# Hybrid attention block on one core: context exponentials of the global attention taken from PSUM under a running maximum, with query scaling, gate-weight rounding and context factors on POOL

## The chip, the core and the metric

The kernel runs on one core of a Trainium2 chip. The metric is the device time of one execution in microseconds, the median over several executions. A profiled execution gives a page and a trace; its span runs from the first to the last instruction.

## What is computed

The reference is one layer of a diffusion backbone with 1024 latent tokens, 256 context tokens and a model width of 1024. The latent tokens pass an input projection, three token mixers in parallel (windowed attention, branch 0; global attention, branch 1; a bidirectional recurrence, branch 2), a gated merge, an output projection and a feed-forward network. The change concerns the two attentions, most of all the global one. Each has 8 query heads in two groups of four that share a key and value head, a head width of 64, and 1280 keys for the global one: 256 of the context and then the 1024 latent ones.

```python
def dense_attn(q, k, v, sink=None):
    ...
    s = jnp.einsum('bqkgd,bjkd->bkgqj', q.reshape(B_, Lq, KV, G, hd), k).astype(jnp.float32) * hd ** -0.5
    ...
    p = jax.nn.softmax(s, axis=-1)[..., :k.shape[1]].astype(v.dtype)
    return jnp.einsum('bkgqj,bjkd->bqkgd', p, v).reshape(B_, Lq, HQ * hd)

def global_attn(q, k, v, ck, cv):
    ...
    k_all = jnp.concatenate([ck, k], axis=1)
    v_all = jnp.concatenate([cv, v], axis=1)
```

The gates of the merge are a plain projection of the normed tokens, 24 units of 128 output channels. The kernel computes them as filler work beside the other stages.

## The kernel before

All work is float32. A product of two float32 tensors is made from three matmuls: each operand is split into a rounded high part (`wh`, `hh`, `ph`, `KH`, written by a cast) and a low part, the difference (`wl`, `hl`, `pl`, `KL`, written by a subtraction on DVE).

The stages run one after another: modulation and norms, the recurrence (branch 2), the token-major projections, then the windowed attention, called stage A here (about 700 to 890 us of the span), the global attention, stage B (about 890 to 1210 us), then merge, output projection and feed-forward network. Stages A and B are one function, `attention`, called with `br` 0 and 1.

In each, a lead part loads keys and values (`prep`) and the first two queries (`qprep`). Then 16 iterations follow, one for each of 8 query tiles of 128 tokens and 2 head groups. In an iteration three generators are woven: `scores(it + 1)`, which makes the probabilities of the next iteration, `values(it)`, which multiplies the present ones with the values, and some steps of the gate units (`gz`, three matmuls a step). The names in the traces:

- `qf`, `qs`, `pq`, `QT`: a query tile as loaded, scaled and split, transposed in PSUM, and copied to SBUF.
- `sa` (stage A), `sbc` and `sbl` (stage B): scores in PSUM. In B, `sbc` holds the context scores of all four heads (128 x 1024) and `sbl` the latent scores of one head. Both take turns in the two buffers of one PSUM tag.
- `pw` in A, `pc` and `plat` in B: the exponentials. In A they are multiplied by the reciprocal sum on POOL (L1405). In B the reciprocal is broadcast to `yT_r` on POOL (L1446), turned by two matmuls into `pr`, copied to `ytmp_R` on ACT (L1316), and multiplied into the result `yT` (L1341).
- `pp`: four transposes of one key tile's probabilities into one PSUM bank. ACT casts it to `ph` (L1323), DVE subtracts to `pl` (L1324), and `po` accumulates values times `ph` and `pl` (L1305, L1306).
- `pq`, `pp` and `pr` take turns in the two banks of PSUM tag "a"; `po` and `gz` in those of tag "b".

In B, before the change, ACT copies the context scores from PSUM to `pc` as they are (L1424). When a head's latent maximum is known, DVE joins it with the context maximum (L1436), and ACT makes both exponentials under the common maximum (L1438 from PSUM, L1439 from `pc`). `values` goes through the two context tiles first and then through the eight latent ones.

A gate unit loads a weight (`wr`, 128 x 1024), ACT casts it to `wh` (L175), DVE subtracts to `wl` (L176). `wh` and `wl` have three buffers each.

The order on each engine is set when the program is built: a list scheduler takes priorities, buffers and its own costs, and so moves instructions of other engines too when one operation changes. At run time each engine goes through its list in order.

Of the kernel before, what the change touches and what calls it, by code (L numbers as in the profile page):

```python
# [12 lines left out]
AF = mybir.ActivationFunctionType  # L13
ALU = mybir.AluOpType
# [4 lines left out]
P = 128  # L19
# [72 lines left out]
def build(tc, ins, out, dbg=None):  # L92
    nc = tc.nc
    V, A, G, T, SP = nc.vector, nc.scalar, nc.gpsimd, nc.tensor, nc.sync
    with ExitStack() as top:
# [66 lines left out]
        cnt = [0]  # L162

        wprio = [0]

        def w_unit(src, nk, ncol, lo_eng=None):

            cnt[0] += 1
            n = nk * ncol
            with tc.high_priority(offset=wprio[0]):  # L170
                raw = wp.tile([P, 1024], F32, tag="wr", name=f"wr{cnt[0]}", bufs=WR)
                SP.dma_start(raw[:, :n] if len(src.shape) == 2 else raw[:, :n].rearrange("p (k n) -> p k n", k=nk), src)
                hi = wp.tile([P, 1024], F32R, tag="wh", name=f"wh{cnt[0]}", bufs=WH)
                lo = wp.tile([P, 1024], F32R, tag="wl", name=f"wl{cnt[0]}", bufs=WL)
                A.copy(hi[:, :n], raw[:, :n])  # L175
                (lo_eng or V).tensor_tensor(out=lo[:, :n], in0=raw[:, :n], in1=hi[:, :n].bitcast(F32),  # L176
                                            op=ALU.subtract)
            return (hi[:, :n].rearrange("p (k n) -> p k n", k=nk),
                    lo[:, :n].rearrange("p (k n) -> p k n", k=nk))
# [1046 lines left out]
def attention(tc, nc, ap_, br, ins, kv_d, q_d, y_d, mm2, bank, ident, identr, fill_gen, fill_steps):  # L1229
    V, A, G, T, SP = nc.vector, nc.scalar, nc.gpsimd, nc.tensor, nc.sync  # L1230

    def tl(shape, tag, nm, bufs=2, dt=F32):
        return ap_.tile(shape, dt, tag=tag, name=f"{tag}{br}_{nm}", bufs=bufs)
# [39 lines left out]
    def qprep(it):  # L1273

        tt, g = divmod(it, 2)
        qf = tl([P, 4, 64], "qf", f"q{it}")
        SP.dma_start(qf, q_d[tt][:, g * 256:(g + 1) * 256])
        qs = tl([P, 4, 2, 64], "qs", f"q{it}", dt=F32R)
        A.activation(qs[:, :, 0], qf, AF.Copy, scale=QSCALE)
        V.scalar_tensor_tensor(out=qs[:, :, 1], in0=qf, scalar=QSCALE, in1=qs[:, :, 0].bitcast(F32),  # L1280
                               op0=ALU.mult, op1=ALU.subtract)
        pq = bank("a", f"pq{br}{it}", (P, 4, P), F32R)
        for h in range(4):
            T.transpose(pq[:, h], qs[:, h].rearrange("p a b -> p (a b)"), identr)
        QT = tl([P, 4, P], "QT", it, 3, F32R)
        A.copy(QT, pq)
        QTs[it] = QT
# [8 lines left out]

    def values(it, PT, kts):
        tt, g = divmod(it, 2)
        Rs = None
        po = bank("b", f"po{br}{it}", (P, 4, P))  # L1300
        prev = []

# [3 lines left out]
            T.matmul(po, vv, pl, start=False, stop=n == len(kts) - 1)  # L1306

        for n, kt in enumerate(kts):
            if it in rs and n == 2:

                r = rs.pop(it)
                pr = bank("a", f"pr{br}{it}", (P, 2, P))
                for a in range(2):
                    T.matmul(pr[:, a], r[:, a * P:(a + 1) * P], ident, start=True, stop=True)
                Rs = tl([P, 2, P], "ytmp", f"R{it}")
                A.copy(Rs, pr)  # L1316
            pp = bank("a", f"pp{br}{it}{kt}")
            for h in range(4):
                T.transpose(pp[:, h], PT(h, n), ident)  # L1319
            ph = tl([P, 4, P], "ph", f"{it}{kt}", PV_BUF, F32R)  # L1320
            pl = tl([P, 4, P], "pl", f"{it}{kt}", PV_BUF, F32R)
            with tc.high_priority(offset=V_PRIO):
                A.copy(ph, pp)  # L1323
                V.tensor_tensor(out=pl, in0=pp, in1=ph.bitcast(F32), op=ALU.subtract)  # L1324
# [12 lines left out]
        for r in range(2):  # L1337
            sl = slice(r * 64, r * 64 + 64)
            V.tensor_tensor(out=yT[sl], in0=pv_[sl, :, r], in1=tmp[sl], op=ALU.add)
        if Rs is not None:  # L1340
            V.tensor_tensor(out=yT, in0=yT, in1=Rs, op=ALU.mult)  # L1341
# [69 lines left out]
def softmax_global(nc, tl, mm2, g, nm, QT, KH, KL, res, rs):  # L1411
# [1 line left out]
    V, A, G, T = nc.vector, nc.scalar, nc.gpsimd, nc.tensor  # L1413
    it = int(nm.split("_")[0])

    st = tl([P, 5, 4], "st", nm)
    nc_, ng, sm, r = st[:, 0], st[:, 1], st[:, 2:4], st[:, 4]
    pc = tl([P, 4, 256], "pc", nm)
    sc = mm2(f"sbc{nm}").rearrange("p a (b c) -> p (a b) c", b=2)
    for h in range(4):  # L1420
        T.matmul(sc[:, h], QT[:, h], KH[:, g, :256], start=True, stop=False)
        T.matmul(sc[:, h], QT[:, h], KL[:, g, :256], start=False, stop=True)
    V.tensor_reduce(out=nc_, in_=sc, axis=AX.X, op=ALU.max, negate=True)
    A.copy(pc, sc)  # L1424
    yield
    Pl = []
    for h in range(4):
# [11 lines left out]
        A.activation(pc[:, h], pc[:, h], AF.Exp, bias=n1, accum_out=sm[:, 0, h:h + 1])  # L1439
        Pl.append(pl)  # L1440
        if h < 3:
            yield
    V.tensor_tensor(out=r, in0=sm[:, 0], in1=sm[:, 1], op=ALU.add)
    V.reciprocal(r, r)
    rb = tl([P, 4, 64], "yT", f"r{nm}")
    G.tensor_copy(rb, r[:, :, None].to_broadcast([P, 4, 64]))  # L1446
# [127 lines left out]
```

## Time and profile before

| what | value |
| --- | --- |
| median of 3 runs | 2118.31 us (2118.1 to 2120.41) |
| the profiled execution's own time | 2119.41 us |
| its span | 2117.6 us |
| PE (matmuls) busy | 2078.3 us, 98% |
| DVE busy | 1379.4 us, 65% |
| ACT busy | 1003.0 us, 47% |
| POOL busy | 289.7 us, 14% |
| granted TensorE clock, mean | 0.996 |

A row of a group names line, engine, operation, output, inputs and shape, and then the durations. A row of a timeline has start, duration, engine, line and operation; in brackets stands how long the engine was idle before it and what released it. PE matmuls are pipelined: a 128x512 one reads 0.39 us in the rows, while the next starts about 0.23 us after it. So the starts, and not the durations, tell what PE needs.

### The profile page before, as it was taken

Reading aid. Unit: us, or ns where it says so; the run is one execution under the profiler, and the core shown is the slowest. Engines: PE = TensorE matmul, PEld = TensorE weight load, DVE = VectorE, ACT = ScalarE, POOL = GpSimd, SP = SyncE. Lnnn points to the kernel's source line nnn. Section 1 sums busy time; section 2 is a strip of 40 time slices with the busy share of each in tenths; the row PEclk is TensorE's granted clock in tenths of the full one; section 3 lists DMA queues with packets and bytes.
Section 4 is the critical chain, followed back from the end, with each engine's and each line's share of the span. In section 5 each row is a group of like instructions: output and inputs, shape, how many; then the busy total and the mean of one; then the engine's idle time right before and its main releaser. Section 6 shows DMA issues by size and latency. Waiting matters only on the chain.

```text
span 2117.6 us, 30402 instructions
## 1 busy us (share of the span) xinstructions
PE 2078.3 (98%) x11622; PEld 1735.2 (82%) x11622; DVE 1379.4 (65%) x2299; ACT 1003.0 (47%) x1760; POOL 289.7 (14%) x257
## 2 busy tenths in 40 slices
PE   7999999999999999999999999999999999999997
PEld 4888888888988788888888788888888888888887
DVE  4736756636565788677887747569777777664423
ACT  4333323311122877688888734346444444453322
POOL 0000000010022222100000000011333344100111
PEclk9999999999999999999999999999999999999999
DMA  9511111136644221211110454541322222295332
GB/s 364 205 44 36 46 50 32 50 113 201 195 139 134 85 60 53 81 45 33 36 33 28 133 188 147 192 151 49 100 86 84 90 71 89 80 304 192 108 124 85
DMA packets 95489, 229.66 MB, mean 108 GB/s; under 512 B 10736, under 2 KB 35696, under 8 KB 94320
## 3 DMA queue, kind: packets, MB, share of 16 engines
q1 hardware_dynamic: 95344, 227.72, 32.4%
q8 instruction: 91, 1.49, 0.3%
q14 instruction: 54, 0.44, 0.1%
HBM read 182.07 MB, written 45.61 MB: 108 GB/s over the span
## 4 chain that ended last, share of the span: by engine, by line
PE 69%; DVE 3%; ACT 2%; issue 1%; POOL 1%; DMA 1%; DVEq 0%; ACTq 0%; POOLq 0%; SPq 0%
PE pp L1319 5%; PE gz L199 3%; PE gz L200 3%; PE gz L201 3%; PE dn L929 3%; PE dn L930 3%; PE dn L928 3%; PE up L852 2%; PE up L853 2%; PE up L854 2%; PE po L1305 2%; PE po L1306 2%; PE br L200 2%; PE br L201 2%; PE br L199 2%; PE upc L854 2%
## 5 line engine op out<-in xcount | busy, mean ns | idle before, releaser
L175 ACT CAST wh<-wr 128x1024 fp32r<-128x1024 f32 (+1 forms) x139 | 145.1, 1045 | 397.7 <-PE dn L929 71.8
L176 DVE TENSOR_TENSOR wl<-wr,wh 128x1024 fp32r<-128x1024 f32 (+1 forms) x139 | 171.2, 1232 | 226.5 <-ACT wh L175 217.4
L1324 DVE TENSOR_TENSOR pl<-pp,ph 128x512 fp32r<-128x512 f32 x236 | 159.5, 688 | 30.4 <-ACT ph L1323 25.0
L199 PE MATMUL gz<-hh,wh 128*128 128x512 f32 x384 | 156.7, 409 | 2.8 <-ACT gs L523 2.8
L200 PE MATMUL gz<-hl,wh 128*128 128x512 f32 x384 | 152.8, 398 | 0.0
L201 PE MATMUL gz<-hh,wl 128*128 128x512 f32 x384 | 152.6, 398 | 0.0
L1323 ACT CAST ph<-pp 128x512 fp32r<-128x512 f32 x236 | 135.7, 585 | 33.6 <-PE pp L1319 31.1
L210 PE MATMUL tm<-wl,hh 128*128 128x256 f32 x384 | 109.0, 284 | 3.4 <-DVE wl L176 3.4
L211 PE MATMUL tm<-wh,hl 128*128 128x256 f32 x384 | 108.8, 283 | 0.0
L209 PE MATMUL tm<-wh,hh 128*128 128x256 f32 x384 | 108.8, 283 | 0.0
L1305 PE MATMUL po<-ph,VHL 128*128 128x512 f32 x236 | 106.4, 451 | 1.7 <-ACT ph L1323 1.1
L929 PE MATMUL dn<-ac,wh 128*128 128x512 f32 x256 | 99.7, 390 | 0.0
L930 PE MATMUL dn<-ac,wl 128*128 128x512 f32 x256 | 99.6, 389 | 0.0
L928 PE MATMUL dn<-ac,wh 128*128 128x512 f32 x256 | 99.6, 390 | 0.0
L1306 PE MATMUL po<-pl,VHL 128*128 128x512 f32 x236 | 98.0, 415 | 0.1
L199 PEld LDWEIGHTS gz<-hh,wh 128*128 128x128 f32 x384 | 73.0, 190 | 16.5 <-ACT gs L523 5.0
L201 PEld LDWEIGHTS gz<-hh,wl 128*128 128x128 f32 x384 | 72.9, 190 | 15.2
L200 PEld LDWEIGHTS gz<-hl,wh 128*128 128x128 f32 x384 | 73.2, 191 | 11.5
L210 PEld LDWEIGHTS tm<-wl,hh 128*128 128x128 f32 x384 | 73.7, 192 | 4.4 <-DVE wl L176 4.0
L1319 PE MATMUL pp<-ident,plat 128*128 128x128 f32 x512 | 77.1, 274 | 0.0
L1319 PEld LDWEIGHTS pp<-ident,plat 128*128 128x128 f32 x512 | 63.2, 141 | 17.0 <-DVE pl L1324 1.2
L733 ACT ACTIVATE u<-c,cw 128x1024 f32<-128x1024 f32 x38 | 47.3, 1246 | 61.9 <-DVE c L889 33.1
(1402 smaller groups left out, 5899.8 us busy)
## 6 DMA issues: line engine op xcount, KB each, us to landing
wr<-in_w_cm SPq DMA_DIRECT2D x48, 512.0 KB, 3.7
wr<-in_w_up SPq DMA_DIRECT2D x44, 512.0 KB, 3.6
wr<-in_w_down SPq DMA_DIRECT2D x33, 512.0 KB, 3.6
wmr<-in_w_mod SPq DMA_DIRECT2D x32, 512.0 KB, 4.6
gate_d<-gs SPq DMA_DIRECT2D x48, 256.0 KB, 2.0
sgt<-gate_d SPq DMA_DIRECT2D x24, 512.0 KB, 3.3
act_d<-u SPq DMA_DIRECT2D x22, 512.0 KB, 2.6
st<-act_d SPq DMA_DIRECT2D x44, 256.0 KB, 4.2
```

Of the source, the lines that this page charges most:

```text
L175: A.copy(hi[:, :n], raw[:, :n])
L176: (lo_eng or V).tensor_tensor(out=lo[:, :n], in0=raw[:, :n], in1=hi[:, :n].bitcast(F32), op=ALU.subtract)
L199: T.matmul(psl, wh[:, k, c], hh[:, k0 + k, cols], start=s, stop=False)
L200: T.matmul(psl, wh[:, k, c], hl[:, k0 + k, cols], start=False, stop=False)
L201: T.matmul(psl, wl[:, k, c], hh[:, k0 + k, cols], start=False, stop=e)
L210: T.matmul(psl, hh[:, k, toks], wl[:, k % 4, :], start=False, stop=False)
L928: T.matmul(z, w[0][:, c], h[0], start=s, stop=False)
L929: T.matmul(z, w[0][:, c], h[1], start=False, stop=False)
L930: T.matmul(z, w[1][:, c], h[0], start=False, stop=e)
L1305: T.matmul(po, vv, ph, start=n == 0, stop=False)
L1319: T.transpose(pp[:, h], PT(h, n), ident)
L1324: V.tensor_tensor(out=pl, in0=pp, in1=ph.bitcast(F32), op=ALU.subtract)
```

## The change

1. In stage B the context exponentials are made straight from the PSUM scores, under the context maximum alone (four instructions with their sums). The copy to `pc` and the later exponentials from `pc` are gone. When all four latent maxima are known, a factor `f`, the exponential of context maximum less common maximum, is made for four heads at once. POOL multiplies `pc` by it, DVE multiplies the context sums by it.
2. `values` in B goes through the eight latent tiles first and the two context tiles last.
3. In B, the broadcast reciprocal is turned at the end of `values`, and DVE multiplies `yT` with it from PSUM. The copy `ytmp_R` on ACT is gone.
4. In A and B, the scaled query is made on POOL instead of ACT.
5. For the 14 gate units that are the filler of stages A and B, the cast to `wh` runs on POOL instead of ACT. All other weights keep ACT.

```diff
@@ w_unit
-                A.copy(hi[:, :n], raw[:, :n])
+                if hi_on[0] is None:
+                    A.copy(hi[:, :n], raw[:, :n])
+                else:
+                    hi_on[0].tensor_copy(hi[:, :n], raw[:, :n])
@@ build, around the two calls of attention
+        hi_on[0] = G
         n0 = 10 + GATES_A
...
         hpool.close()
+        hi_on[0] = None
@@ qprep
-        A.activation(qs[:, :, 0], qf, AF.Copy, scale=QSCALE)
+        G.tensor_scalar(out=qs[:, :, 0], in0=qf, scalar1=QSCALE, scalar2=1.0, op0=ALU.mult, op1=ALU.mult)
@@ values
-            if it in rs and n == 2:
-
-                r = rs.pop(it)
-                pr = bank("a", f"pr{br}{it}", (P, 2, P))
-                for a in range(2):
-                    T.matmul(pr[:, a], r[:, a * P:(a + 1) * P], ident, start=True, stop=True)
-                Rs = tl([P, 2, P], "ytmp", f"R{it}")
-                A.copy(Rs, pr)
...
         for e in prev:
             pv(*e)
+        if it in rs:
+            r = rs.pop(it)
+            pr = bank("a", f"pr{br}{it}", (P, 2, P))
+            for a in range(2):
+                T.matmul(pr[:, a], r[:, a * P:(a + 1) * P], ident, start=True, stop=True)
+        else:
+            pr = None
...
-        if Rs is not None:
-            V.tensor_tensor(out=yT, in0=yT, in1=Rs, op=ALU.mult)
+        if pr is not None:
+            V.tensor_tensor(out=yT, in0=yT, in1=pr, op=ALU.mult)
@@ softmax_global
     V.tensor_reduce(out=nc_, in_=sc, axis=AX.X, op=ALU.max, negate=True)
-    A.copy(pc, sc)
+    for h in range(4):
+        A.activation(pc[:, h], sc[:, h], AF.Exp, bias=nc_[:, h:h + 1], accum_out=sm[:, 0, h:h + 1])
...
         A.activation(pl, sf, AF.Exp, bias=n1, accum_out=sm[:, 1, h:h + 1])
-        A.activation(pc[:, h], pc[:, h], AF.Exp, bias=n1, accum_out=sm[:, 0, h:h + 1])
...
-    V.tensor_tensor(out=r, in0=sm[:, 0], in1=sm[:, 1], op=ALU.add)
+    V.tensor_tensor(out=f, in0=ng, in1=nc_, op=ALU.subtract)
+    A.activation(f, f, AF.Exp)
+    for h in range(4):
+        G.tensor_scalar(out=pc[:, h], in0=pc[:, h], scalar1=f[:, h:h + 1], scalar2=1.0, op0=ALU.mult, op1=ALU.mult)
+    V.tensor_tensor(out=r, in0=sm[:, 0], in1=f, op=ALU.mult)
+    V.tensor_tensor(out=r, in0=r, in1=sm[:, 1], op=ALU.add)
     V.reciprocal(r, r)
...
-    res[it] = ((lambda h, n: pc[:, h, n * P:(n + 1) * P] if n < 2 else Pl[h][:, (n - 2) * P:(n - 1) * P]),
-               list(range(10)))
+    res[it] = ((lambda h, n: Pl[h][:, n * P:(n + 1) * P] if n < LT else pc[:, h, (n - LT) * P:(n - LT + 1) * P]),
+               [2 + n for n in range(LT)] + [0, 1])
```

How the instructions move, at three places. Lines of the changed kernel are some lines on: L1307 and L1308 are the two `po`, L1313 is `pp`, L1329 is `pr`, L1422 and L1423 are `sbc`, L1287 is `pq`, L203 is `gz`.

PE in stage B, at the end of an iteration, before (the last two latent tiles, `ph_78` and `ph_79`, of iteration 7, then the scores of iteration 9):

```order
L1305 MATMUL po_10369<-ph_78_10524,VHL_0_8531 128x512
L1421 MATMUL sbc__10570<-KH_0_8529,QT_9_10354 128x256
L1422 MATMUL sbc__10570<-KL_0_8530,QT_9_10354 128x256
...
L1306 MATMUL po_10369<-pl_78_10525,VHL_0_8531 128x512
L1305 MATMUL po_10369<-ph_79_10538,VHL_0_8531 128x512
L1284 MATMUL pq_10561<-identr,qs_q_10558 128x128 x2
L1306 MATMUL po_10369<-pl_79_10539,VHL_0_8531 128x512
L1284 MATMUL pq_10561<-identr,qs_q_10558 128x128 x2
L1421 MATMUL sbc__10570<-KH_0_8529,QT_9_10354 128x256
...
L1319 MATMUL pp_10582<-ident,pc_8__10357 128x128 x4
```

And with the change (iteration 6 ends with the context tiles `ph_60` and `ph_61`, then the scores of iteration 8):

```order
L1307 MATMUL po_10187<-ph_60_10343,VHL_0_8531 128x512
L1422 MATMUL sbc__10392<-KH_0_8529,QT_8_10169 128x256
L1423 MATMUL sbc__10392<-KL_0_8530,QT_8_10169 128x256
L1308 MATMUL po_10187<-pl_60_10344,VHL_0_8531 128x512
L1307 MATMUL po_10187<-ph_61_10357,VHL_0_8531 128x512
L1329 MATMUL pr_10367<-ident,yT_r__10100 128x128
L1308 MATMUL po_10187<-pl_61_10358,VHL_0_8531 128x512
L1329 MATMUL pr_10367<-ident,yT_r__10100 128x128
...
L1422 MATMUL sbc__10392<-KH_0_8529,QT_8_10169 128x256
L1423 MATMUL sbc__10392<-KL_0_8530,QT_8_10169 128x256
L1313 MATMUL pp_10407<-ident,plat_7_0_10223 128x128
```

Two of the eight `sbc` matmuls, where four were, now stand ahead of the last `po`; `pr` has come to this place; all four `pq` and six `sbc` stand between the last `po` and the first `pp` of the next iteration. In the odd iterations one more `sbc` and one `gz` stand there too.

ACT in stage B after that place, with the change (L1336 and L1337 copy `po`, L1289 is the copy `QT`, L1317 the cast `ph`, L1426 the new exponentials, L1440 a latent exponential):

```order
L1336 COPY ytmp_7_10587<-po_10406 64x256
L1337 COPY ytmp_7_10587<-po_10406 64x256
L1289 COPY QT_10_10604<-pq_10599 128x512
L1317 CAST ph_82_10628<-pp_10623 128x512
L1426 ACTIVATE pc_9__10607,st_9__10606<-sbc__10608,st_9__10606 128x256 x3
L1317 CAST ph_83_10640<-pp_10635 128x512
L1426 ACTIVATE pc_9__10607,st_9__10606<-sbc__10608,st_9__10606 128x256
L1317 CAST ph_84_10661<-pp_10656 128x512
L1440 ACTIVATE plat_9_0_10651,st_9__10606<-sbl_0_10644,st_9__10606 128x1024
```

Where one copy of the context scores stood, four exponentials now read them, and one `ph` stands between the third and the fourth.

POOL in stage A, iteration 3, with the change (L179 is the cast to `wh`, L1282 the scaled query, L1406 the product that makes `pw`):

```order
L1406 TENSOR_SCALAR pw_3_0_6581<-pw_3_0_6581,st_3__6575 128x640
L1406 TENSOR_SCALAR pw_3_1_6619<-pw_3_1_6619,st_3__6575 128x640
L179 CAST wh_7642<-wr_7640 128x1024
L1406 TENSOR_SCALAR pw_3_2_6646<-pw_3_2_6646,st_3__6575 128x640
L1282 TENSOR_SCALAR qs_q_7011<-qf_q_7009 128x4x64
L1406 TENSOR_SCALAR pw_3_3_6673<-pw_3_3_6673,st_3__6575 128x640
```

Before, the four L1405 stood there alone.

More of the change, by code (lines that the diff above doesn't have):

```diff
@@ L164, in build @@
         wprio = [0]
+        hi_on = [None]
         def w_unit(src, nk, ncol, lo_eng=None):
@@ L1298, in values @@
         tt, g = divmod(it, 2)
-        Rs = None
         po = bank("b", f"po{br}{it}", (P, 4, P))
@@ L1414, in softmax_global @@
     it = int(nm.split("_")[0])
-    st = tl([P, 5, 4], "st", nm)
-    nc_, ng, sm, r = st[:, 0], st[:, 1], st[:, 2:4], st[:, 4]
+    st = tl([P, 6, 4], "st", nm)
+    nc_, ng, sm, r, f = st[:, 0], st[:, 1], st[:, 2:4], st[:, 4], st[:, 5]
     pc = tl([P, 4, 256], "pc", nm)
```

## The prediction

> **What bounds the kernel now.** I read the page's busy line first, then busy time and PE's waits by stage, and then one period of stage B in order of time.
>
> ```profile
> PE 2078.3 (98%) x11622; PEld 1735.2 (82%) x11622; DVE 1379.4 (65%) x2299; ACT 1003.0 (47%) x1760; POOL 289.7 (14%) x257
> ...
> 700.00:890.00 190.00, 185.68 (x1090) 156.39 (x1090) 147.57 (x455) 144.54 (x361) 49.83 (x64) 1.00 0.20 60
> 890.00:1210.00 320.00, 316.95 (x1813) 259.07 (x1812) 252.91 (x420) 263.06 (x556) 6.44 (x16) 0.99 0.15 50
> ...
> PE pp L1319 <- POOL pw L1405: 1.5, 5, 0.6
> PE pq L1284 <- DVE qs_q L1280: 1.4, 1, 1.4
> PE po L1305 <- ACT ph L1323: 0.8, 1, 0.8
> PE gz L199 <- ACT gs L523: 0.5, 1, 0.5
> ...
> PE pr L1314 <- DVE pl L1324: 1.8, 4, 1.0
> ```
>
> The columns of a stretch are start and end, length, then the busy time of PE, PEld, DVE, ACT and POOL, the granted clock and DMA. PE is idle for 190 - 185.68 = 4.3 us of stage A and 320 - 316.95 = 3.05 us of B. In the lists of PE's waits (stage A above, B below) the named ones come to 4.2 us and about 2.5 us. ACT is busy 263 of 320 us in B and DVE 253: neither is full. So the 1.8 us or so that the change takes off ACT in a period of B is no gain by itself. Time comes only from PE's waits, from PE's own order, or it is lost to waits that the new order makes.
>
> ```profile
> 1002.65 0.29 PE L1284 MATMUL pq<-identr,qs_q 128*128 128x128 f32 x2
> 1002.78 0.47 PE L1306 MATMUL po<-pl,VHL 128*128 128x512 f32 x1
> 1003.08 0.29 PE L1284 MATMUL pq<-identr,qs_q 128*128 128x128 f32 x2
> 1003.21 0.35 PE L1421 MATMUL sbc__9929<-KH,QT 128*128 128x256 f32 x1
> 1003.40 0.27 PE L1422 MATMUL sbc__9929<-KL,QT 128*128 128x256 f32 x1
> 1003.51 0.28 PE L1421 MATMUL sbc__9929<-KH,QT 128*128 128x256 f32 x1
> ...
> 1003.75 0.60 PE L1319 MATMUL pp<-ident,pc__9716 128*128 128x128 f32 x4
> 1004.11 0.47 PE L199 MATMUL gz<-hh,wh 128*128 128x512 f32 x1
> 1004.42 0.39 PE L200 MATMUL gz<-hl,wh 128*128 128x512 f32 x1
> 1004.64 0.39 PE L201 MATMUL gz<-hh,wl 128*128 128x512 f32 x1
> ...
> 1007.38 0.68 PE L1314 MATMUL pr<-ident,yT_r__9861 128*128 128x128 f32 x4 [0.29 <-DVE pl L1324]
> 1007.82 0.48 PE L1305 MATMUL po<-ph,VHL 128*128 128x512 f32 x1
> ```
>
> Here I go by starts. A 128x512 matmul takes PE 0.22 to 0.23 us (1004.42 to 1004.64), four transposes 0.36 (1003.75 to 1004.11), a 128x256 one 0.11 to 0.12. The first 128x512 behind transposes takes 0.31 (1004.11 to 1004.42): a switch from transposes costs 0.31 - 0.22 = 0.09 us. The last row but one shows `pr` held by a bank that DVE had not yet left.
>
> ```profile
> 1003.28 0.37 ACT L1335 COPY ytmp<-po 64x256 f32<-64x256 f32 x1 [1.48 <-PE po L1306]
> 1004.06 0.59 ACT L1286 CAST QT<-pq 128x512 fp32r<-128x512 f32 x1
> 1006.21 1.01 ACT L1424 COPY pc__9928<-sbc__9929 128x1024 f32<-128x1024 f32 x1
> ...
> 1004.95 1.23 DVE L1423 TENSOR_REDUCE st__9927<-sbc__9929 128x4 f32<-128x1024 f32 x1
> 1006.21 0.42 DVE L1341 TENSOR_TENSOR yT<-yT,ytmp_R 128x256 f32<-128x256 f32 x1
> ...
> L1439 ACT ACTIVATE pc__8742<-pc__8742,st__8741 x4: 497/498/518, 906.0 to 912.7; 128x256 f32<-128x256 f32 x4
> L1316 ACT COPY ytmp_R<-pr x16: 370/373/378, 919.0 to 1195.2; 128x256 f32<-128x256 f32 x16
> L1279 ACT ACTIVATE qs_q<-qf_q x32: 410/421/463, 698.0 to 1116.7; 128x256 fp32r<-128x256 f32 x32
> L1446 POOL COPY yT_r__9009<-st__8859 x1: 403/403/403, 928.1 to 928.1; 128x256 f32<-128x256 f32 x1
> ...
> L1446 POOL COPY yT_r__11984<-st__11838 x1: 403/403/403, 1189.0 to 1189.0; 128x256 f32<-128x256 f32 x1
> ```
>
> This is ACT and then DVE in the same period. The broadcasts give the period: (1189.0 - 928.1) / 14 = 18.64 us.
>
> **The change part by part**, against the profiled execution of 2119.41 us.
>
> *ACT in B.* The copy (1.01), `ytmp_R` (0.37) and the query (0.42) go: 1.8 us a period. The four context exponentials stay, 0.50 each, with another source and place. The exponential of the factor is new, at most one of theirs. All of it lies beside PE and counts zero; were the cover gone, ACT's 263 us would have to reach 317.
>
> *Fewer switches.* The two orders have 119 and 199 switches from transposes to other matmuls in A and B before, 111 and 190 after. 17 fewer at 0.09: **-1.5 us**. Bounds 0 and -1.5.
>
> *`pr` at the end.* It no longer cuts in between the first tiles: the 1.8 us of its four waits go. One of these, 1.0, stands in the last iteration. **-1.8**, bounds -1.8 and 0.
>
> *Queries and `wh` on POOL, stage A.*
>
> ```profile
> L1405 POOL TENSOR_SCALAR pw<-pw,st__6724 128x640 f32<-128x640 f32 x4 | 3.2, 809 | 6.3 <-DVE st__6724 L1400 5.2 <-DVE st__6724 L1403 0.7 <-ACT ph L1323 0.4
> L1405 POOL TENSOR_SCALAR pw<-pw,st__8212 128x512 f32<-128x512 f32 x4 | 2.8, 700 | 7.3 <-PE sa L1389 4.1 <-DVE st__8212 L1403 3.3
> L581 POOL COPY tbA<-cs 128x512 f32<-128x512 f32 x2 | 1.2, 612 | 34.1 <-DMA cs<-in_rope 34.1
> L145 POOL CAST identr<-ident 128x128 fp32r<-128x128 f32 x1 | 0.3, 291 | 3.9 <-DMA ident<-in_ident 3.9
> L1137 POOL COPY S<-S x8: 614/1501/1512, 180.6 to 415.0; 64x512 f32<-64x512 f32 x8
> ```
>
> 809 less 700 ns for 128 more elements is 0.85 ns an element, so the scaled query of 256 is about 0.49 us. 612 less 291 for 384 elements is 0.84, so a `wh` cast of 1024 is about 1.04 us (estimates from these rows). Stage A gets 16 x 0.49 + 7 x 1.04 = 15 us on a POOL busy 49.8 of 190. Before the four products of an iteration POOL idles 6.3 us, 1.6 each, so one cast or query fits into each gap. `pp` waits for what is queued behind it, the third and fourth `pw`. If no gap were free, six casts in such places would cost up to 6 us; if ACT's relief brought `pw` earlier, the 1.5 us of waits would go. I take **-0.5**, near the second, since the gaps are longer than what is put into them.
>
> The wait of 1.4 us at the start of A is for the second query. Its load stands behind the key tiles, whose buffers ACT frees, and ACT loses the casts there. **-1.0**, bounds -1.4 and 0 (the transfer itself may set it).
>
> *The new order at the end of an iteration of B.* Call t0 the start of the last `po` (1002.78 above). The two `po` copies start 0.50 after it, `QT` starts at 1.28 and ends at 1.87. With the change PE needs behind t0: `po` 0.30, half of `pr` 0.22, four `pq` 0.26, six `sbc` 0.72; so it asks for the first `pp` at 1.5. The two "a" banks are then held by `pr`, until DVE's multiply at 1006.21 + 0.42, or t0 + 3.85, and by `pq`, until `QT`. So `pp` waits 1.87 - 1.5 = 0.37 us in even iterations, and about nothing in odd ones, where a `gz` and an `sbc` (0.35) come first. Ahead of t0, two `sbc` fewer (0.24) cover the last `pl`, which comes no earlier: on its way the factor and two small DVE operations take the place of one exponential. Against the waits before that is 0 to 0.6 us a period; I take 0.2, half of the one and a little of the other. 15 periods: **+3.0**, bounds 0 and +9.
>
> *The tail of B.* In the last iteration the scores have run out.
>
> ```profile
> 1190.00:1192.00 2.00, 1.09 (x6) 0.53 (x4) 1.66 (x2) 1.96 (x5) 0.00 (x0) 1.00 0.91 295
> 1192.00:1194.00 2.00, 1.68 (x7) 1.53 (x8) 1.96 (x5) 1.10 (x2) 0.00 (x0) 0.61 0.99 342
> 1194.00:1196.00 2.00, 2.00 (x8) 1.71 (x7) 1.79 (x3) 1.28 (x3) 0.00 (x0) 0.54 0.96 371
> ```
>
> PE was idle 0.91 us of two, then the granted clock was 0.61 and 0.54: 2 x 0.39 + 2 x 0.46 = 1.7 us lost. With the change ACT still casts a merge weight there while PE waits for `ph`, so I expect another idle gap and another dip. **-0.5**, bounds -1.7 (no dip) and +1.7 (twice as long).
>
> The Trainium skill, "TensorE: Matmul & The Clock Gate" (the HAM clock gate), says that the clock falls to half after an idle window of about 3.4 us. Here a gap far shorter went ahead of the fall, so the trace decides; by the rule alone the tail's clock would be an accident of the window, and this term zero.
>
> Sum: -1.5 - 1.8 - 0.5 - 1.0 + 3.0 - 0.5 = **-2.3 us**. The profiled execution lies 1.1 above the median of 2118.31, so on the median: 2116.0 us.
>
> **The rivals.**
>
> *The waits go and no new ones come.* PE's 7.3 us of idle time in A and B fall to some 3, `pw` and `QT` come early since ACT is freer, and the dip is gone: -4.3 - 1.5 - 1.7 = -7.5, about **2110.8**. For it: every named wait hangs on ACT or on what ACT delays. Against it: the new `pp` stands 0.37 us before its bank.
>
> *The context scores hold their bank too long: slower.* The second latent `sbl` needs the buffer that `sbc` leaves. Before, that was at 1006.21 + 1.01, t0 + 4.4. Now the reduction ends at t0 + 3.4 and three exponentials (1.5), a `ph` (0.59) and the fourth with its read-out (0.69) follow: t0 + 6.2. In even iterations PE asks for it after about 1.5 + 4.3 (two `pp` and a third 1.07, six `gz` 1.45, four `sbl` 0.92, switches and `po` 0.87) = t0 + 5.8. The wait at `pp` hides this 0.4; whatever else delays the reduction or ACT does not hide. At 0.7 us a period it costs 10.5: 2116.0 - 3.0 + 10.5 = **2123.5**. It turns the sign from about 0.35 us a period on (5.3 us of gains over 15). Against it: ACT has 1.8 us a period more room.
>
> *It changes nothing.* New and old waits balance: **2118.3**.
>
> *POOL and DVE get in each other's way.* L1137 has 64x512 copies of 1.50 us in the median beside one of 0.61: POOL was held 0.9 us. If the casts met that in stage A, `pw` would come 0.9 late in seven iterations, 6.3 us: **2122.3**. Against it: the L1405 rows of one shape stay within 809 and their like. The Trainium skill, "SBUF — State Buffer" (Who interferes with whom), has the rule: a DVE instruction with two SBUF inputs and a POOL instruction that reads SBUF block each other whole. That speaks against moving work to POOL beside `wl`; `pl`, with one input in PSUM, would be free.
>
> **How the numbers follow.** Forecast 0.46, with its own range 2113 to 2120; the first rival 0.26, the second 0.15, no change 0.09, the last 0.04. 0.2% is 4.2 us, about what a measurement tells from none: faster is below 2114.1, slower above 2122.5. A quarter of the forecast's chance lies below 2114.1: faster 0.26 + 0.11 = 0.37. Slower is the second rival and half of the last, 0.17; the rest, 0.46, is the same. The range, 2108 to 2124, leaves out the low end of the first rival and the high half of the second.
>
> **What would show it.** PE's waits in B no longer name `pr`; `pp` waits for `QT` in even iterations, `sbl` for L1426 at most 0.4 us. The period of B is 18.5 to 18.8 us. ACT's busy time in B falls by some 30 us and the span hardly moves. A `pw` that waits behind a cast, or PE waits in B above 6 us in sum, would make the prediction wrong upward; a clock of 1.00 at the end of B downward.

## The result and the profile after

The changed kernel takes 2123.86 us in the median of 9 runs (2121.4 to 2126.05), the kernel before 2119.12 (9 runs, 2117.51 to 2120.41). The ratio is 1.0026, with a 95% interval of 1.0017 to 1.0035: slower by about 5 us. I had forecast 2116.0, so the sign is wrong.

The profiled execution of the changed kernel took 2125.58 us, its span is 2123.8. First the busy line, then stages A and B with the columns of the prediction, then the longest named waits of PE in A (two rows) and in B (the rest).

```profile
PE 2077.6 (98%) x11622; PEld 1734.5 (82%) x11622; DVE 1392.6 (66%) x2331; ACT 961.5 (45%) x1698; POOL 348.7 (16%) x367
...
700.00:890.00 190.00, 184.44 (x1087) 157.09 (x1087) 153.91 (x455) 133.88 (x337) 65.48 (x85) 1.00 0.19 60
890.00:1210.00 320.00, 312.44 (x1791) 254.96 (x1790) 252.91 (x447) 231.43 (x517) 47.73 (x100) 1.00 0.15 47
...
PE pp L1313 <- POOL pw L1406: 4.9, 5, 1.0
PE po L1307 <- ACT ph L1317: 0.4, 1, 0.4
...
PE po L1307 <- ACT ph L1317: 1.8, 2, 1.0
PE pp L1313 <- DVE yT L1342: 1.5, 2, 1.2
PE pq L1287 <- DVE qs_q L1283: 0.8, 1, 0.8
PE pp L1313 <- ACT QT L1289: 0.8, 5, 0.2
PE pp L1313 <- DVE pl L1318: 0.7, 1, 0.7
PE sbl L1433 <- ACT plat L1440: 0.4, 1, 0.4
```

PE's work is the same (11622 instructions), its idle time is not: 5.6 us in A (4.3 before) and 7.6 us in B (3.05 before). ACT's busy time in B fell by 32 us, as expected, and bought nothing. In A the waits for `pw` went from 1.5 to 4.9 us. In B `pr` is gone from the list, and other names have come, five of them among the rows shown; with three smaller rows the list comes to 6.8 us, above the 6 that I had set as a sign against the forecast.

The first and the last context scores mark stage B for PE: the first two rows are the kernel before, the last two the changed one (of a tile's four matmuls, first and last start).

```profile
L1421 PE MATMUL sbc__8743<-KH,QT x4: 278/278/280, 900.4 to 901.6; 128*128 128x256 f32 x4
L1421 PE MATMUL sbc__11840<-KH,QT x4: 278/281/282, 1169.8 to 1171.2; 128*128 128x256 f32 x4
```

```profile
L1422 PE MATMUL sbc__8743<-KH,QT x4: 280/282/351, 902.4 to 903.4; 128*128 128x256 f32 x4
L1422 PE MATMUL sbc__11902<-KH,QT x4: 278/282/365, 1175.7 to 1177.7; 128*128 128x256 f32 x4
```

From 900.4 to 1171.2 are 270.8 us, from 902.4 to 1177.7 are 275.3: B is 4.5 us longer (4.6 to the very last matmul of the context scores). Its period, by the broadcasts on POOL, is (1196.4 - 932.1) / 14 = 18.88 us, 18.64 before. From the first transposed keys of A to B's first context scores it is 0.4 us more, behind B 0.3 less. The 1.8 us more before 40 us in this one profile are not the change's but a dip of the clock: from 15 to 20 us the granted clock is 0.66, and 1.00 in the kernel before. 2 of the 18 kernels below (x_qv, x_q13) show the same dip, 16 do not.

**How the table below is made.** For each matmul I took the time to the next start, less what its shape needs (128x512 0.227, 128x256 0.117, 128x128 0.108 us; the last of a group of transposes together with the one behind it; the transposes of `pq` need less than 0.108, so every kernel's sum is somewhat low). The sum between first and last context scores is PE's time beyond its work in B: 11.6 us before, 15.8 after. Pieces above 0.13 us I count as waits, what is left are small delays between matmuls of different kinds. The column "pw" is what the profile names as `pp` waiting for `pw` in A.

| kernel | what it has | ratio to before (95%) | pw, A | beyond work, B |
| --- | --- | --- | --- | --- |
| before | | 1 | 1.5 | 11.6 |
| changed | parts 1 to 5 | 1.0026 (1.0017 to 1.0035) | 4.9 | 15.8 |
| e1_ctx | 1, 2 | 1.0014 (1.0006 to 1.0023) | 1.5 | 14.8 |
| e2_pr | 3 | 1.0028 (1.0019 to 1.0036) | 1.5 | 17.0 |
| e3_pool | 4, 5 | 1.0018 (1.0010 to 1.0027) | 4.7 | 15.3 |
| e4_nopr | 1, 2, 4, 5 | 1.0054 (1.0042 to 1.0066) | 4.7 | 21.6 |
| e5_ctxpr | 1, 2, 3 | 1.0015 (1.0006 to 1.0024) | 1.5 | 15.8 |
| e6_q | 4 | 0.9995 (0.9984 to 1.0006) | 2.3 | 12.0 |
| e8_prb | all, `pr` in another bank | 1.0123 (1.0107 to 1.0138) | 4.7 | 35.0 |
| c1_slen | none, other order | 0.9995 (0.9986 to 1.0004) | 1.5 | 11.3 |
| x_nowh | 1 to 4 | 1.0003 (0.9994 to 1.0012) | 2.5 | 13.4 |
| x_qv | all, `QT` on DVE | 1.0018 (1.0009 to 1.0027) | 5.1 | 16.0 |
| x_q13 | 4, other order | 0.9996 (0.9987 to 1.0005) | 2.2 | 10.6 |
| x_a13 | all, other order | 1.0032 (1.0021 to 1.0044) | 4.7 | 17.6 |
| z_1in | all, sums with one tensor input | 1.0020 (1.0010 to 1.0029) | 3.4 | 15.7 |
| z_nowh_qv | 1 to 4, `QT` on DVE | 1.0000 (0.9991 to 1.0009) | 2.3 | 12.1 |
| z_nowh_qv_fold | the same, sink sum folded | 1.0009 (1.0000 to 1.0018) | 3.6 | 12.3 |
| z_q13_fold | 4, other order, fold | 0.9990 (0.9982 to 0.9999) | 3.7 | 11.2 |
| w_a | 1 to 4, and 5 for A | 1.0012 (1.0003 to 1.0021) | 3.6 | 14.6 |
| w_b | 1 to 4, and 5 for B | 1.0018 (1.0009 to 1.0027) | 4.3 | 15.8 |

Medians are of 4 to 12 runs each, beside 9 to 31 runs of the kernel before.

### The profile page after: what moved, and what is told of

Same layout as the page of the kernel before. It is cut to its first block, busy times and chain, and to the rows that moved or that the text cites. A ratio compares the mean times of both kernels' runs of the same rounds, so it can differ in the third digit from the quotient of the medians.

```text
span 2123.8 us, 30532 instructions
## 1 busy us (share of the span) xinstructions
PE 2077.6 (98%) x11622; PEld 1734.5 (82%) x11622; DVE 1392.6 (66%) x2331; ACT 961.5 (45%) x1698; POOL 348.7 (16%) x367
## 4 chain that ended last, share of the span: by engine, by line
PE 61%; DVE 2%; ACT 2%; issue 1%; DMA 1%; POOL 1%; DVEq 0%; SPq 0%; POOLq 0%; ACTq 0%
PE pp L1313 5%; PE dn L932 3%; PE dn L931 3%; PE dn L933 3%; PE up L855 2%; PE up L857 2%; PE up L856 2%; PE po L1308 2%; PE po L1307 2%; PE br L204 2%; PE br L205 2%; PE br L203 2%; PE gz L203 2%; PE gz L204 2%; PE gz L205 2%; PE upc L857 2%
## 5 line engine op out<-in xcount | busy, mean ns | idle before, releaser
L177 ACT CAST wh<-wr 128x1024 fp32r<-128x1024 f32 (+1 forms) x125 | 130.3, 1043 | 388.3 <-PE dn L932 70.4
L1317 ACT CAST ph<-pp 128x512 fp32r<-128x512 f32 x236 | 136.2, 586 | 59.8 <-PE pp L1313 58.6
L203 PE MATMUL gz<-hh,wh 128*128 128x512 f32 x384 | 156.2, 407 | 3.6 <-ACT gs L527 3.6
L1307 PE MATMUL po<-ph,VHL 128*128 128x512 f32 x236 | 105.4, 446 | 2.2 <-ACT ph L1317 2.2
L1308 PE MATMUL po<-pl,VHL 128*128 128x512 f32 x236 | 98.4, 417 | 0.4 <-DVE pl L1318 0.4
L203 PEld LDWEIGHTS gz<-hh,wh 128*128 128x128 f32 x384 | 72.8, 189 | 16.7 <-ACT gs L527 5.4
L204 PEld LDWEIGHTS gz<-hl,wh 128*128 128x128 f32 x384 | 72.7, 189 | 11.3
L1313 PE MATMUL pp<-ident,plat 128*128 128x128 f32 x512 | 78.1, 275 | 3.7 <-DVE yT L1342 1.5
L1313 PEld LDWEIGHTS pp<-ident,plat 128*128 128x128 f32 x512 | 61.4, 140 | 23.7 <-ACT QT L1289 4.8
L204 PE MATMUL br<-yl,wh 128*128 128x512 f32 x192 | 75.1, 391 | 0.3 <-DVE yl L1471 0.2
```

Source lines behind the costliest of these rows:

```text
L203: T.matmul(psl, wh[:, k, c], hh[:, k0 + k, cols], start=s, stop=False)
L204: T.matmul(psl, wh[:, k, c], hl[:, k0 + k, cols], start=False, stop=False)
L1307: T.matmul(po, vv, ph, start=n == 0, stop=False)
```

## The experiments

### Which part costs it

Parts 1 and 2, part 3, and parts 4 and 5, each put alone into the kernel before; and the changed kernel with part 3 undone. The edits are the hunks of the diff above, taken singly.

> Parts 1 and 2 alone (context exponentials from PSUM, factor, latents first); the reciprocal's turn stays early with its copy, queries and gate weights stay on ACT. In the changed kernel stage B lost 4.6 us from its first to its last context scores, stage A and its lead together about nothing. Theory 'turn at the end' (pr and pq hold both 'a' banks, pp waits for QT): this kernel has no turn there, so it should be at 2119 +- 1.5, ratio 1.000. Theory 'context part' (context tiles last, their bank held by four exponentials, the factor's small operations ahead of pl on DVE): the loss is here, 2122 to 2124, ratio 1.0015 to 1.0025. Theory 'POOL': 2119.

> Part 3 alone (turn of the reciprocal at the end of values, multiplied from PSUM). Theory 'turn at the end': a pp behind QT costs 0.3 us in each of 15 periods and takes the place of the old waits of pr, which were 1.8 us: 2121 to 2123, ratio 1.001 to 1.002. Theory 'context part': the four waits of pr go and nothing comes, 2117 to 2118.5, ratio 0.999. Theory 'POOL': the same 2117 to 2118.5.

> Parts 4 and 5 alone (scaled query and 14 gate weights on POOL). In the changed kernel pp waited 4.9 us for pw in stage A (1.5 before), the wait of 1.4 for the second query was gone, and the first query of stage B came 0.8 late. Theory 'turn at the end' and theory 'context part': these balance to +0 to +2, 2119 to 2121. Theory 'POOL': all of the loss, 2122.5 to 2124.5, with most of it in stage B, where queries on POOL come later.

> The changed kernel with part 3 undone: the turn is made early again, at the third key tile, and copied by ACT. Theory 'turn at the end': B's loss of 4.6 us goes, 2119 to 2120.5, ratio 1.000 to 1.0007. Theory 'context part': it stays, 2123 to 2125, ratio 1.002 to 1.003; the waits at the iteration's end change their names only. Theory 'POOL': it stays too.

No theory had this: each part alone is slower (1.0014, 1.0028, 1.0018), and their sum, 0.6%, is more than twice the whole, 0.26%. Undoing part 3 does not help, it doubles the loss (1.0054). With the context part and POOL's work in place (e4_nopr), `pr` at the early spot waits in 12 iterations, 7.3 us in sum, where the kernel before had 2.0. So part 3 is a loss alone and a gain beside the others; the parts can't be priced singly, and why part 3 alone costs so much was not followed up. Both theories that name one part for B fell.

### The POOL parts taken apart, and a control

```diff
 e6_q     (before, and only:)
-        A.activation(qs[:, :, 0], qf, AF.Copy, scale=QSCALE)
+        G.tensor_scalar(out=qs[:, :, 0], in0=qf, scalar1=QSCALE, scalar2=1.0, op0=ALU.mult, op1=ALU.mult)
 e5_ctxpr (changed, with the ACT query, and:)
-        hi_on[0] = G
+        hi_on[0] = None
 e8_prb   (changed, and:)
-            pr = bank("a", f"pr{br}{it}", (P, 2, P))
+            pr = bank("b", f"pr{br}{it}", (P, 2, P))
 c1_slen  (before, and:)
-S_LEN = 1.35
+S_LEN = 1.3
```

> Part 4 alone (scaled query on POOL). In the run with parts 4 and 5 alone DVE waited 11.1 us for POOL's scaled query in stage B (2.5 for ACT's before), with pl queued behind. Theory 'the query on POOL stalls DVE': this shows here again, some 10 us of DVE waits, B 3 to 5 us longer than before, 2120 to 2122. Rival 'the gate weights on POOL did it': B as before within 1 us, 2118 to 2119.

> Parts 1, 2 and 3 without the POOL parts 4 and 5; PE's list at the iterations' ends is that of the changed kernel. Theory 'the order at the end costs it': the pp waits of 0.2 to 0.3 us a period stay and B stays 3.5 to 5 us longer than before: 2121.5 to 2123.5. Rival 'the POOL parts cost it': B within 1.5 us of before, 2118 to 2120.

> The changed kernel with the turn of the reciprocal in a bank of the other tag, that of po and gz. In the changed kernel pp waited 0.23 to 0.32 us in 12 periods of stage B, 3.3 us in sum, while pr and pq held both 'a' banks. Theory 'a banks held': these waits go below 0.1 us each and the time falls by 3 us or so from the 2123.9 of the changed kernel, to 2120 to 2121.5 (ratio 1.0005 to 1.0013). Rival 'the bank only names the wait' (a wait for po or gz, which share their banks with pr then, takes its place): 2123 to 2126, ratio 1.002 to 1.0035.

> A control: the kernel before with one number of the weave altered (1.30 for 1.35, the share of steps that scores take), so the same instructions on the same engines in another order in stage B. Theory 'the old order is a narrow optimum' (any other order of B brings waits of 0.1 to 0.3 us a period): 2120 to 2123, ratio 1.001 to 1.002. Rival 'order does not matter at this size, the parts of the change do': 2118 to 2119, ratio 1.000.

The control is at 0.9995, and its PE list is another one in stage B: that the order differs is no loss by itself. The query on POOL is free, though DVE stands still for it as the theory said; this row is e6_q's, DVE's waits in B:

```profile
DVE qs_q L1283 <- POOL qs_q L1282: 13.9, 13, 3.3
```

13.9 us of waits of an engine with work behind them, and PE does not see them: the theory "the query on POOL stalls DVE" fell. e3_pool less e6_q leaves the gate weights: 0.23%. In e5_ctxpr the waits of `pp` at the iteration's end stay, and so does B's loss. e8_prb came out far worse than even its rival: `gz` and `po` now wait for DVE's `yT`, 3.5 and 2.4 us, and much else with them. The list of all engines is another, so it says nothing of the "a" banks.

### The gate weights off POOL; the wait for QT taken away

```diff
 x_nowh (changed, and:)
-        hi_on[0] = G
+        hi_on[0] = None
 x_qv   (changed, and:)
-        A.copy(QT, pq)
+        (A.copy if br == 0 else V.tensor_copy)(QT, pq)
 x_q13  (e6_q with S_LEN = 1.3)      x_a13  (changed, with S_LEN = 1.3)
```

> The changed kernel with part 5 undone: the 14 gate weights are cast on ACT again, the queries stay on POOL. Theory 'gate weights on POOL hold pw': pp's waits for pw in stage A fall from 4.9 us to between 1.5 and 2.5, A gets 2 to 3 us shorter, B stays some 4 us longer than before: 2121 to 2122, ratio 1.0010 to 1.0016. Rival 'the casts cost nothing': 2123 to 2124.5, ratio 1.002 to 1.003.

> The changed kernel with the copy QT of stage B on DVE instead of ACT, where it stands behind the two copies of po (0.37 each). Theory 'pp waits for a bank that QT leaves late': on DVE the copy (about 0.69, as pl of the same shape) can start as soon as the four pq are done, some 0.4 us earlier, and the 12 pp waits of 0.23 to 0.32 us shrink below 0.1: 2120.5 to 2122, ratio 1.0008 to 1.0016. Rival 'the pp wait only stands where other delays of the same place would be seen' (small pieces of pr, pq, sbc and po between one another, DVE's own queue): 2123 to 2126, ratio 1.002 to 1.0035.

> Part 4 alone (scaled query on POOL) together with the weave number 1.30 of the control: each of the two was at 0.9995 of before. If their gains are of separate places they add: 2116 to 2117.5, ratio 0.9985 to 0.9992. Rival 'one order's luck doesn't carry over to another': 2118 to 2120, ratio 0.9997 to 1.0006.

> The changed kernel with the weave number 1.30: the same instructions in another order in stage B; six or seven sbc still stand behind the last po in the even iterations, with four transposes of pq and one of pr. Theory 'the chain at the iteration's end (po, its copies, QT, pp) costs it whatever the weave': B stays 3.5 to 5.5 us longer than before, 2122.5 to 2125. Rival 'the loss is a bad draw of the scheduler': B within 2 us of before, 2119 to 2121.

x_nowh is at 1.0003: without the 14 casts on POOL the change costs nothing that can be measured. The difference to the changed kernel is 0.23%, the same as between e3_pool and e6_q, 4.9 us both times. The casts are not the only way to lose, though: e5_ctxpr has none on POOL and is at 1.0015. It differs from x_nowh by the scaled query alone, which it has on ACT; the two intervals overlap, and whether the query on POOL helps beside parts 1 to 3 is not shown. In x_qv the regular waits of `pp` for `QT` (12 pieces, 3.3 us) are gone, and the ratio went from 1.0026 to 1.0018, with intervals that overlap; three single waits of 1.3 to 1.5 us, two of them of `pp` for `QT` on its new engine, and small pieces came in their place (beyond work 16.0 and 15.8). x_q13 is not faster than either of its halves. In x_a13 the weave number that was harmless in the kernel before makes the changed one no better: the loss is not one bad draw of the scheduler.

### Why a cast on POOL is late and makes others late

The trace shows it in place. This is stage A of the changed kernel in order of time, in the iteration of 842 us (POOL, DVE, and the `pp` that waits):

```profile
841.39 1.04 POOL L179 CAST wh<-wr 128x1024 fp32r<-128x1024 f32 x1 [1.80 <-PE gz L204]
841.45 0.99 DVE L1401 TENSOR_TENSOR st__7913<-snk,st__7913 128x1 f32<-128x1 f32 x1
...
842.71 0.50 DVE L1403 TENSOR_TENSOR st__7913<-st__7913 128x1 f32<-128x1 f32 x1 [0.27 <-ACT st__7913 L1402]
...
843.14 1.21 DVE L180 TENSOR_TENSOR wl<-wr,wh 128x1024 fp32r<-128x1024 f32 x1
...
844.27 0.15 DVE L1404 RECIPROCAL st__7913<-st__7913 128x1 f32<-128x1 f32 x1
...
844.61 0.80 POOL L1406 TENSOR_SCALAR pw<-pw,st__7913 128x640 f32<-128x640 f32 x1 [1.41 <-DVE st__7913 L1404]
...
845.47 0.76 PE L1313 MATMUL pp<-ident,pw 128*128 128x128 f32 x5 [1.02 <-POOL pw L1406]
```

The cast waits 1.80 us for the third `wh` buffer, which PE's `gz` frees. While it runs, DVE's sum of 128 numbers takes 0.99 us, in the kernel before it takes 0.15 (rows below). Then `wl`, which is made from the cast's result, stands between the next sum and the reciprocal. `pw` comes 1.0 us late, not behind the cast in POOL's queue, but by way of DVE. B has the same:

```profile
968.89 1.05 POOL L179 CAST wh<-wr 128x1024 fp32r<-128x1024 f32 x1
969.97 1.42 DVE L180 TENSOR_TENSOR wl<-wr,wh 128x1024 fp32r<-128x1024 f32 x1 [1.61 <-POOL wh L179]
971.31 0.85 DVE L1340 TENSOR_TENSOR yT<-po,ytmp 64x256 f32<-64x256 f32 x2
972.19 1.23 DVE L1424 TENSOR_REDUCE st__9518<-sbc__9520 128x4 f32<-128x1024 f32 x1
973.45 0.42 DVE L1342 TENSOR_TENSOR yT<-yT,pr 128x256 f32<-128x256 f32 x1
973.92 0.66 PE L1313 MATMUL pp<-ident,plat 128*128 128x128 f32 x4 [1.15 <-DVE yT L1342]
...
1024.58 1.04 POOL L179 CAST wh<-wr 128x1024 fp32r<-128x1024 f32 x1 [16.40 <-PE gz L204]
1024.72 0.91 DVE L1449 TENSOR_TENSOR st__9953<-st__9953 128x4 f32<-128x4 f32 x1
1025.76 0.66 DVE L1318 TENSOR_TENSOR pl<-pp,ph 128x512 fp32r<-128x512 f32 x1
1026.48 0.51 PE L1308 MATMUL po<-pl,VHL 128*128 128x512 f32 x1 [0.39 <-DVE pl L1318]
```

In the first, DVE stands 1.61 us for the cast, and the multiplication that gives back the bank of `pr` queues behind `wl`; in the second a sum of 128x4, 0.16 in most iterations, takes 0.91, and `pl` comes that much later. In x_nowh neither wait of PE stands between the first and the last context scores. To tell "held off" from "queued behind", I gave the small sums of stage A one tensor input and left their place:

```diff
 z_1in (changed, and:)
-            V.tensor_tensor(out=sk[:, b], in0=snk[:, bs], in1=ng[:, b], op=ALU.add)
+            V.tensor_scalar(out=sk[:, b], in0=ng[:, b], scalar1=snk[:, bs], scalar2=None, op0=ALU.add)
...
-            V.tensor_tensor(out=sm[:, b], in0=sm[:, b], in1=sk[:, b], op=ALU.add)
+            V.tensor_scalar(out=sm[:, b], in0=sm[:, b], scalar1=sk[:, b], scalar2=None, op0=ALU.add)
 z_nowh_qv      (x_nowh and x_qv together)
 z_nowh_qv_fold (the same) and z_q13_fold (x_q13), each with:
-            V.tensor_tensor(out=sk[:, b], in0=snk[:, bs], in1=ng[:, b], op=ALU.add)
-            A.activation(sk[:, b], sk[:, b], AF.Exp)
+            A.activation(sk[:, b], ng[:, b], AF.Exp, bias=snk[:, bs])
```

> The changed kernel with the two small DVE sums of stage A's softmax (128x1) written with one tensor input and a per-partition number instead of two tensor inputs. Theory 'POOL's cast holds off a DVE operation with two inputs in SBUF': their longest durations fall from 0.99 to about 0.2 us, pp's waits for pw in stage A from 4.9 to 2 or less, stage A by 2 to 3 us, 2120.5 to 2122, ratio 1.0010 to 1.0018. Rival 'DVE's order costs it' (wl, 1.21, between the sum and the reciprocal): the waits for pw stay at 4 to 5 us, 2123 to 2124.5, ratio 1.002 to 1.003.

> The changed kernel without part 5 (gate weights on ACT again), and with the copy QT of stage B on DVE. Without part 5 it was at 1.0003, with 13 pp waits in B of 3.8 us in sum; QT on DVE took such waits away in the changed kernel and the time fell by 1.8 us. If the two are separate: 2117 to 2118.5, ratio 0.9994 to 1.0000. Rival 'the waits come back elsewhere at the same place': 2119 to 2120.5, ratio 1.0002 to 1.0010.

> The same, and in stage A the sum of sink and negated maximum is taken into ACT's exponential as its bias, so one small DVE operation and one handover a head less. pw comes some 0.2 us earlier for each head; pp waited 2.5 us for pw in A in the kernel without part 5. Theory 'pw is late by its own chain': 1 to 2 us less than without the fold, ratio 0.9985 to 0.9993. Rival 'the waits for pw come from elsewhere' (what ACT or DVE does first): no difference within 0.7 us.

> Part 4 alone with the weave number 1.30 (0.9996 of before) and the same fold: a candidate to beat both. Theory as before: pp's waits for pw in A (2.2 us) fall by half or more, 2115.5 to 2116.5, ratio 0.9987 to 0.9992. Rival: no difference, 0.9996.

One sum in iteration 12, shortest, median and longest of four in ns, before, changed, and z_1in; behind the last, its waits for `pw` in A:

```profile
L1400 DVE TENSOR_TENSOR st__7913<-snk,st__7913 x4: 138/152/162, 832.3 to 839.3; 128x1 f32<-128x1 f32 x4
```

```profile
L1401 DVE TENSOR_TENSOR st__7913<-snk,st__7913 x4: 151/157/992, 834.5 to 841.4; 128x1 f32<-128x1 f32 x4
```

```profile
L1401 DVE TENSOR_SCALAR st__7913<-st__7913,snk x4: 198/204/207, 832.6 to 839.9; 128x1 f32<-128x1 f32 x4
...
PE pp L1313 <- POOL pw L1406: 3.4, 5, 0.7
```

With one tensor input no sum is held any more, beside the same casts. That is shown. What it is worth is about half: the waits for `pw` fall from 4.9 to 3.4 us, not to 2; from the first to the last score of A it is 1.4 us less, and the ratio, 1.0020, doesn't part from 1.0026. What is left is for the most part the same conflict the other way round: the third `pw` now runs beside `wl`, and it is POOL that is held. These rows are z_1in's, in the same iteration:

```profile
840.76 1.86 POOL L1406 TENSOR_SCALAR pw<-pw,st__7913 128x640 f32<-128x640 f32 x1
840.82 1.23 DVE L180 TENSOR_TENSOR wl<-wr,wh 128x1024 fp32r<-128x1024 f32 x1
...
842.68 0.33 PE L1313 MATMUL pp<-ident,pw 128*128 128x128 f32 x1 [0.70 <-POOL pw L1406]
```

Four `pw` of z_1in take 1.86 us instead of 0.80, one in each of four iterations with a cast; in the changed kernel none does. Behind each of the four PE waits 0.70 us: 2.8 of the 3.4. So the run shows that the sums were held, but it does not part "held off" from "queued behind": with the sums free, `pw` is held in their place, and what `wl`'s place in DVE's queue costs beside that is not shown.

The Trainium skill, "SBUF — State Buffer" (Who interferes with whom), says that a DVE instruction with two SBUF inputs contends with a POOL instruction that reads SBUF, and one with at most one SBUF input does not, outside the modes in which DVE uses both of its port pairs. These rows agree: the sum takes 0.99 us beside the cast with two inputs, and 0.20 with one.

z_nowh_qv came out as if its two gains were separate: 1.0000, beyond work in B 12.1 us, no `pp` wait for `QT` above 0.13 us. The fold fell as a theory: in both kernels that have it the waits for `pw` rose (2.3 to 3.6, and 2.2 to 3.7 us), since the new order puts `wl` beside the fourth `pw`: in each of the two kernels four `pw` take 1.83 us, and PE waits 0.65 us behind each, 2.6 us in sum, though neither casts on POOL. z_q13_fold has the lowest ratio of all, 0.9990 (0.9982 to 0.9999). As the lowest of 19, with an interval that ends at 0.9999 and overlaps that of x_q13, it is not shown to beat the kernel before, and the reason I gave for it is not the reason.

### Which stage's casts

```diff
 w_a (w_b: br == 1)
         for br, units in ((0, gates[10:n0]), (1, gates[n0:])):
+            hi_on[0] = G if br == 0 else None
```

> The changed kernel with only stage A's seven gate weights cast on POOL, B's on ACT. Without any it was at 1.0003, with all fourteen at 1.0026. Theory 'the cost is B's' (a cast that waits for its buffer holds DVE's wl, and the sums of the factor take 0.9 us beside it): 2119.5 to 2121, ratio 1.0004 to 1.0011, B's time as without casts. Rival 'the cost is A's' (pp waits for pw 4.9 us instead of 2.5): 2121.5 to 2123, ratio 1.0014 to 1.0022.

> The changed kernel with only stage B's seven gate weights cast on POOL, A's on ACT. Theory 'the cost is B's': 2121.5 to 2123, ratio 1.0015 to 1.0022, B some 2 to 3 us longer than without casts. Rival 'the cost is A's': 2119.5 to 2121, ratio 1.0004 to 1.0011.

Without casts 1.0003, A's alone 1.0012, B's alone 1.0018, both 1.0026: 0.09% and 0.15% add up to the whole. So both seem to have a share; the intervals are too wide to say which is larger. The cut is not clean: with B's casts alone `pp` still waits 4.3 us for `pw` in A, since B's first gate weights are loaded while A runs.

## Why the prediction was wrong, step by step

- **Queries and `wh` on POOL, stage A: -0.5. This step failed, and it carries the sign.** I looked for the price in POOL's own queue (is there a gap before the third `pw`?), in stage A only, took the low side of a range from -1.5 to +6, and gave B's seven casts no price at all. Measured: the casts cost 0.23% in one pair of kernels (x_nowh and changed) and 0.23% in another (e6_q and e3_pool), 4.9 us. Of that, 2.4 us are waits for `pw` in A (4.9 against 2.5 in x_nowh) and 2.4 us are in B (15.8 against 13.4 beyond work). The way is through DVE and not through POOL's queue: `wl` waits for the cast, small sums with two inputs take 0.9 to 1.0 us beside it, and what stands behind them on DVE is late. How the price divides between these two is not shown. The queries alone were free (e6_q).
- **POOL and DVE get in each other's way: a rival at 0.04.** Its mechanism is the one that z_1in shows, with DVE as the one that is held. I had it against `pw`, a long operation on POOL, and argued that its rows stay at 0.8 us. In the changed kernel they do; the short operations on DVE do not. In z_1in, where these sums are free, four rows of `pw` go to 1.86. So the kind of loss was named, on the other engine, and the chance was too small.
- **Fewer switches: -1.5. This failed too: they are worth about 0.3 us.** In these rows of the kernel before I had the 0.09 us behind the transposes and not the other half:

```profile
1056.73 0.38 PE L1319 MATMUL pp<-ident,plat 128*128 128x128 f32 x2
1056.87 0.47 PE L1305 MATMUL po<-ph,VHL 128*128 128x512 f32 x1
1057.18 0.39 PE L1306 MATMUL po<-pl,VHL 128*128 128x512 f32 x1
...
1059.84 0.60 PE L1319 MATMUL pp<-ident,pc__10357 128*128 128x128 f32 x4
1060.19 0.48 PE L199 MATMUL gz<-hh,wh 128*128 128x512 f32 x1
1060.51 0.39 PE L200 MATMUL gz<-hl,wh 128*128 128x512 f32 x1
```

  Two transposes take 0.14, four take 0.35: 0.105 each, and the last one of a group only 0.035. So 0.07 of the 0.09 had been given before. 17 switches at 0.02 are 0.3 us.
- **`pr` at the end: -1.8. Right, and more.** Above 0.1 us each, `pr` waited 2.0 us in the kernel before, and another 1.7 stood beside `pq` at the end of iterations (six pieces of 0.25 to 0.32). In the changed kernel one of these last, of 0.29, is left.
- **New waits at the end: +3.0. Right in name, and in size partly by luck.** `pp` waits for a bank in 12 periods, about 0.2 to 0.32 us, 3.3 us in sum. This is an odd iteration of the changed kernel; ACT's three copies stand in the order that I read:

```profile
1081.99 0.60 PE L1329 MATMUL pr<-ident,yT_r__10537 128*128 128x128 f32 x4
1082.35 0.36 PE L1422 MATMUL sbc__10826<-KH,QT 128*128 128x256 f32 x1
1082.56 0.39 PE L1308 MATMUL po<-pl,VHL 128*128 128x512 f32 x1
1082.78 0.46 PE L1287 MATMUL pq<-identr,qs_q 128*128 128x128 f32 x4
1083.06 0.37 ACT L1336 COPY ytmp<-po 64x256 f32<-64x256 f32 x1
...
1083.45 0.37 ACT L1337 COPY ytmp<-po 64x256 f32<-64x256 f32 x1
1083.84 0.59 ACT L1289 CAST QT<-pq 128x512 fp32r<-128x512 f32 x1
1083.98 0.39 PE L203 MATMUL gz<-hh,wh 128*128 128x512 f32 x1
1084.48 0.66 PE L1313 MATMUL pp<-ident,plat 128*128 128x128 f32 x4
```

  In the even iterations the waits are about 0.3 us, where I had 0.37. I expected about nothing in the odd ones; here `pp` starts at 1084.48, when `QT` is done, 0.50 behind a `gz` that needs 0.23. What I left out are small pieces: in x_nowh those under 0.13 us come to 9.2 us in B, before to 6.8. No single place in these rows explains them: the `sbc` behind `pr` takes 0.21 where 0.12 would do, but some 0.07 of that was given before, as at the switches above. They are spread over many kinds of neighbours. The `pp` waits of x_nowh, 3.8 us, take the place of the 3.7 of old ones; the 2.4 more of small pieces are why B is not shorter with ACT 26 us freer. What they hang on was not tried.
- **The second query, A's lead: -1.0. Right**, but its like came back: PE's wait for a query, 1.4 us in A's lead before, is not in A's list after, and 0.8 us of it is in B's.
- **The tail: -0.5, with another dip of the clock. Near in size, by luck.** Behind the last context scores it is 0.35 us less in the two profiles, but in another way: no dip and longer gaps. In these stretches of the changed kernel PE is idle 0.87, 0.56 and 1.03 of two us, and the clock stays:

```profile
1196.00:1198.00 2.00, 1.13 (x6) 0.54 (x4) 1.62 (x2) 1.67 (x4) 0.82 (x3) 1.00 0.99 352
1198.00:1200.00 2.00, 1.44 (x8) 1.03 (x8) 1.96 (x4) 1.63 (x2) 0.00 (x0) 1.00 0.94 336
...
1202.00:1204.00 2.00, 0.97 (x6) 0.63 (x5) 0.82 (x1) 1.90 (x3) 0.00 (x0) 1.00 0.84 217
```

- **The second rival, 2123.5, hit the number and not the cause.** `sbl` waits for ACT 0.4 us in all of B, once. A right time is no proof of a mechanism.

Measured terms, changed kernel against before, from the two profiles: A with its lead +0.37, B +4.58, behind it -0.35, in sum 4.6 us. The medians differ by 4.7 us; 0.26% of 2118 is 5.5.

## What to carry to other kernels

An operation that moves to another engine takes its waits with it. For a cast that waits for a buffer, price the consumers of its result (here `wl` on DVE), what queues behind those, and what the engine it joins (here POOL) does to DVE's operations with two SBUF inputs. When one side of such a conflict is freed, look at the rows of the other side, which may now be the one held. Parts of a change to a kernel that is bound by one engine at 98% can't be priced alone: here three losses of 0.14 to 0.28% made one of 0.26%, and leaving one out made it 0.54%.

A cost per switch between two kinds of work has to be taken over both sides of the switch, not from the slow instruction behind it.

## What the runs showed of the hardware

- A DVE sum of 128x1 with two SBUF inputs takes 0.15 us alone and 0.99 beside a POOL cast of 1.04; with one tensor input 0.20, and at most 0.22 beside the cast.
- It goes both ways: `wl` (two inputs) takes 1.42 and 1.52 us beside POOL instead of 1.22, the scaled query on POOL takes 1.37 us beside `wl`, where half of its 32 rows take 0.41 or less (I had estimated 0.49), and `pw` on POOL takes 1.86 us beside `wl` in z_1in instead of 0.80.
- A dip of the clock is a stretch of about 3.4 us at half: the granted clock is 0.51 from 1192.4 to 1195.8 us in the kernel before, and 0.50 from 15.8 to 19.2 in the changed one. At the end of B the kernel before has a dip behind a gap of 0.96 us in PE's work. Seven other kernels have gaps there whose longest is 1.02 to 1.37 us, and no dip; e8_prb has one later, behind a gap of 3.40 us. So one profile of 20 kernels shows it at this place, and nothing ties it to the change. What decides it stays open.
